# Three places for the values on their way out, and an earlier time for the second block's statistics, in the prologue of a two-layer diffusion transformer kernel

## The chip, the cores and the metric

The kernel runs on one core of one Trainium2 chip. The metric is the device time of one execution in microseconds; the time of a kernel is the median of its runs. Besides the runs there is one profiled execution, whose trace gives every instruction's start and length. The engines are PE (matrix products; PEld is its weight load), DVE (vector), ACT (scalar, activations), POOL (GpSimd) and SP, which in this kernel issues every DMA.

## The reference

The reference computes two transformer layers over 1024 latent tokens (a grid of 16 x 64) and 256 context tokens of width 1024, in float32. Layer 0 mixes by neighbourhood attention with 16 heads of 64, layer 1 by grouped-query attention. Only the start of layer 0 bears on this change:

```python
mod_l = (silu_c @ ada_w[i] + ada_b[i])[:, None, :]
sh1_l, sc1_l, g1_l, sh2_l, sc2_l, g2_l = jnp.split(mod_l, N_MOD, axis=-1)
a_l = ada_norm(h, norm_mix[i], sh1_l, sc1_l)      # rms_norm(x, g) * (1 + scale) + shift
...
qkv = a_l @ w_qkv                                  # split into q, k, v
s_nb = q_r . k_b * scale + bias                    # bias gathered from rpb
p = softmax(concat(s_nb, s_cx)); o = p @ v
y_lat = o @ w_o
...
h = h + g1_l * y_l
h = h + g2_l * swiglu_ffn(ada_norm(h, norm_ffn[i], sh2_l, sc2_l), ffn_w_in[i], ffn_w_out[i])
```

The context tokens go through the same steps with modulation vectors of their own.

## The kernel before

All matrix operands are split into a high part, rounded to the fp32r format of PE, and a low part that holds the rest, so a product takes three matmuls: high by high, low by high, high by low. Names ending in `h` and `l` are these parts (`ah`/`al` of the activations, `wh`/`wl` of the weights, `qh`/`ql` of q and k). Making the high part is a cast on ACT, making the low part a subtraction on DVE or POOL.

Tokens lie in three blocks: block 0 and block 1 are 512 latent tokens each, block 2 is the context with 256. Activations are kept with the width on the partitions, as eight slices `kc` of 128 by the block's tokens.

The prologue, `startup()`, does the following for layer 0 and for the first two heads' q and k and the first four heads' v:

- `loads()` starts all input DMAs in a fixed order, on SP.
- `stat(b)` squares the eight slices of block b on ACT (line 364; the first two are `nacc` and `nacb`, the others `nsq` with two places), adds them up on DVE (slices 2, 4, 5, 7) and POOL (slices 3, 6) at line 367, sums over partitions with a matmul pair by a matrix of ones (line 374, tile `ms`), and takes Ln and Exp on ACT (lines 377, 378) for the reciprocal root `nrs`.
- `modulation(m)` and `shift(m, w)` make the modulation vectors (lines 396, 397, 409 to 419).
- `apply0(kc)` (lines 429 to 433) and `apply(b, kc)` (lines 441, 442 and `norm_lo`, lines 131 to 134) normalize a slice: DVE makes `nx`, ACT makes `ah`, and the low part `al` is made by DVE for even slices and by POOL for odd ones, where it takes two rows (lines 131 and 132). `nx` has three places.
- `split(k, pool)` makes `wh` on ACT (line 337) and `wl` on DVE (line 339) for a weight tile; the values' weights are the two tiles `v0` and `v1`.
- `projections()` issues PE's work: q and k of block 0 (lines 781 to 783), values of tiles 0 to 3, q and k of block 1, values of tiles 4 and 5, q and k of the context block, values of tiles 8, 9, 6, 7. A tile of values is 128 tokens.
- `proj_v` makes one tile of values (lines 797 to 799) and sends it out: the cast on ACT (line 803) and the subtraction on DVE (line 804) fill a tile `vt`, and a DMA stores it in DRAM (`Vd`). The q and k parts go out in the same way from `qh` and `ql` (lines 823, 825; `Kd`, `Qd`).
- `bias_steps()` has SP issue 24 DMAs that spread the relative bias table into `E`, and 16 that gather it into `Bd`. They stand in SP's queue between the stores.

Every step of the prologue is a Python generator that yields how long, in microseconds of an assumed clock, it takes until the next step. `startup` keeps them in a heap by that clock, and the order in which they are popped is the order in which the instructions are issued on each engine. Each engine runs its instructions in that order and waits at the head of its queue for what that instruction needs. The clock decides the order alone, not the time. The start times are these:

```python
for at, gen in [(0.0, loads()), (5.0, c_rows()), (10.0, stat(0)), (CFG["t1"], stat(1)), (CFG["t2"], stat(2)), (28.0, projections())] + \
        [(CFG["ts"], shifts_ctx())] + \
        [(max(9.5, a), modulation(m)) for m, a in enumerate((7.0, 13.0, 18.0, 22.0, 25.0, 28.5, 31.5, 34.5))]:
    start(at, gen)
```

Tiles come from pools. With `bufs=2` a name has two places, which are used in turn; an instruction that writes a tile waits until whatever read or wrote the tile that last had the place is done, a store by DMA included.

After the prologue the attention of layer 0 runs by a written table (ORDERA and ORDERB), with the remaining projections and the modulation for later (`adaw`, line 503) put between by `Lanes`. Softmax blocks `Pt` are scaled by POOL (line 871), transposed on PE (line 878) and multiplied by the values (line 508). SP's place for each DMA there comes from the order in which the program, on its assumed clock, finds it ready.

Of the kernel before, what the change touches and what calls it, by code (L numbers as in the profile page):

```python
# [11 lines left out]
F32R = mybir.dt.float32r  # L12
# [6 lines left out]
P = 128  # L19
# [12 lines left out]

V_NMIX, V_NFFN, V_NFIN, V_B, V_QG, V_KG, V_C = 0, 16, 32, 40, 136, 137, 138
V_N = 154
CFG = dict(lag=3, tv=5.0, tm=5.0, t1=40.0, t2=55.0, ts=43.0, p0=28, lo="GD", n=39, ra=2.3, rc=0.7, rq=1.1, rb=1.05, gap=263, r1=1.262, lh=300, tk='ADAG', tb=1000000000.0, tg=1, lp='GD')
PERIOD1 = 8172
ORDER1 = {
# [35 lines left out]
def _build(tc, nc, I, O, top):  # L73
# [193 lines left out]
    def startup():  # L267

        ET = mybir.EngineType
        with ExitStack() as ph:  # L270
# [10 lines left out]
            def start(at, gen):  # L281

                heapq.heappush(todo, (at, next(count), gen))
# [10 lines left out]
            def load_raw(k, src):  # L294
                raws[k] = wraw.tile([P, D], F32, name="wr")
                if k[0] == "v":
                    dma(out=raws[k][:].rearrange("p (u n) -> p u n", u=2), in_=src.rearrange("u p n -> p u n"))
                else:
                    dma(out=raws[k][:], in_=src)

            def loads():
# [12 lines left out]
                for i in range(2):  # L314
                    load_raw(f"v{i}", W[16:18, :, i * 512:i * 512 + 512])
                    start(now + CFG["tv"], split(f"v{i}", w0))
                    yield 1.5
# [15 lines left out]
            def split(k, pool):  # L333
                hi = pool.tile([P, D], F32R, name="wh")
                lo = pool.tile([P, D], F32R, name="wl")
                ws[k] = hi, lo
                s.copy(hi[:], raws[k][:])
                yield 1.2
                v.tensor_tensor(lo[:], raws[k][:], hi[:].bitcast(F32), ALU.subtract)
# [4 lines left out]
            def c_rows():  # L344
                for w in range(2):
                    for i in range(2):
                        ps = psm.tile([P, 512], F32, name="ps1")
                        dg = tmp.tile([P, 4, P], F32, name="nsq", bufs=2)
                        v.tensor_tensor(dg[:], ident[:].unsqueeze(1).broadcast_to([P, 4, P]),
                                        silc2[:, 4 * i:4 * i + 4, w:w + 1].broadcast_to([P, 4, P]), ALU.mult)  # L350
                        t.matmul(ps[:], lhsT=ones[:], rhs=dg[:].rearrange("p a n -> p (a n)"), start=True, stop=True)
                        yield 0.8
                        s.mul(crow[w][:, i * 512:i * 512 + 512], ps[:], float(D))
                        yield 0.3

            def stat(b):
                n = BLK[b][1]
                acc = []
                for kc in range(KC):
# [10 lines left out]
                    yield 0.55  # L370
                yield CFG["tm"] if b == 1 else 2.0
                ms = psp.tile([P, 512], F32, name="ms")
# [26 lines left out]
            def shifts_ctx():  # L399

                for m in range(4, KC):
                    shift(m, 1)
                    yield 1.6
# [43 lines left out]
            def first_qk(b):  # L447
# [3 lines left out]
                for kc in range(KC):  # L451
                    while (b, kc) not in ready or b == 0 and min(kc + CFG["lag"], KC - 1) not in ready:
                        yield 0.2
# [7 lines left out]
            def vals0(tiles):  # L461
                for c in proj_v(psm, tmp, [ws["v0"], ws["v1"]], Vd[0], tiles):
                    yield c * 0.64
# [91 lines left out]
    class Lanes:  # L555
# [170 lines left out]
        def tick(self, cost=1.0):  # L726

            self.now += 650
            for e in "TML" + CFG["tk"]:
                if self.busy.get(e, 0) < self.now + CFG["tg" if e == "G" else "tb"]:  # L730
# [55 lines left out]
    def proj_v(psm, pool, ws, dst, tiles=range(10)):  # L786


        for tb in tiles:
            b = min(tb // 4, 2)  # L790
            ah, al = acts[b]
            c = slice((tb % 4) * P, (tb % 4) * P + P)
            ps = psm.tile([P, 512], F32, name="ps1")
            out = ps[:, :256]
            for kc in range(KC):
                hi, lo = (w.rearrange("p (u k n) -> p k u n", u=2, n=P)[:, kc % 4] for w in ws[kc // 4])
                t.matmul(out, lhsT=ah[:, kc, c], rhs=hi, start=kc == 0, stop=False)
                t.matmul(out, lhsT=al[:, kc, c], rhs=hi, start=False, stop=False)
                t.matmul(out, lhsT=ah[:, kc, c], rhs=lo, start=False, stop=kc == KC - 1)
                yield 0.5  # L800
            vt = pool.tile([P, 4, P], F32R, name="vt", bufs=2)
            pv = out.rearrange("p (h d) -> p h d", d=HD)
            s.copy(vt[:, :, 0:HD], pv)
            v.tensor_tensor(vt[:, :, HD:], pv, vt[:, :, 0:HD].bitcast(F32), ALU.subtract)
            dma(out=dst[:, :, tb, :].rearrange("h p d -> p h d"), in_=vt[:])
# [985 lines left out]
    with ExitStack() as ph:  # L1791
# [260 lines left out]
        n = CFG["n"]  # L2052
# [604 lines left out]
```

## Time and profile before

| | us |
|---|---|
| three runs | 3013.36, 3013.57, 3020.36 |
| median | 3013.57 |
| profiled execution | 3018.95 |
| its span, first to last instruction | 3017.1 |
| PE busy in the span | 2915.8 (97%) |
| DVE, ACT, POOL busy | 2300.5, 1621.0, 1238.8 |
| granted clock of PE over the span | 0.992 |

The rows of the trace are read as follows: the start in us from the span's start, the length in us, the engine, the line of the program, the operation, what it writes and reads, its shape, and how many rows are merged (x2). In brackets stands the idle time of the engine just before, and what ended it. Rows on an engine may overlap by about 0.1 us, since an instruction starts while the one ahead drains. SPq are the DMAs that SP issues; the length there is the time of issue, not of the transfer.

### The profile page before, as it was taken

The numbers are of one execution on the slowest core, as the hardware profiler recorded it, in microseconds if no ns is written. First come the engines' busy times: TensorE is split into PE (matmuls) and PEld (weight loads), VectorE is DVE, ScalarE is ACT, GpSimd is POOL, SyncE is SP. The second block draws the span as 40 slices with busy tenths as digits, with TensorE's granted clock in tenths as the row PEclk, the third lists the DMA queues.
The fourth block names the chain that finished last, engine by engine and source line by source line (L and its number), as shares of the span: only waits on it lengthen the run. The fifth ranks groups of instructions, "written<-read, shape, count | busy, mean of one in ns | idle before, by whom it ended". The sixth has DMA issues, their size and how long they took to land.

```text
span 3017.1 us, 50132 instructions
## 1 busy us (share of the span) xinstructions
PE 2915.8 (97%) x16460; PEld 2503.3 (83%) x16460; DVE 2300.5 (76%) x4671; ACT 1621.0 (54%) x3739; POOL 1238.8 (41%) x1105
## 2 busy tenths in 40 slices
PE   7999998999999999999999899999999999999998
PEld 5788997888788888888888788888888878888886
DVE  7478778876798875557777588999887887776776
ACT  4345545776742222234456489899887632333444
POOL 4246556776145451121121256666643354223112
PEclk9999999999999999999999999999999999999999
DMA  7777777887545562249656523333323343224962
GB/s 268 217 223 239 227 217 230 239 244 219 187 147 188 194 225 76 93 152 324 211 192 205 164 83 95 112 98 102 107 75 127 133 140 122 102 105 149 324 217 108
DMA packets 309218, 519.03 MB, mean 172 GB/s; under 512 B 46560, under 2 KB 113248, under 8 KB 308320
## 3 DMA queue, kind: packets, MB, share of 16 engines
q1 hardware_dynamic: 308960, 515.84, 52.7%
q8 instruction: 131, 2.15, 0.3%
q14 instruction: 127, 1.04, 0.1%
HBM read 389.61 MB, written 120.18 MB: 169 GB/s over the span
## 4 chain that ended last, share of the span: by engine, by line
PE 77%; DVE 10%; DMA 4%; ACT 3%; POOL 2%; issue 2%; SPq 1%; DVEq 0%; ACTq 0%; POOLq 0%
PE pf L1472 9%; PE pf L1474 9%; PE pf L1473 9%; PE T L878 5%; PE o L508 5%; PE pf L1721 5%; PE pf L1720 5%; PE pf L1722 5%; PE ps L781 3%; PE ps L783 3%; PE ps L782 3%; PE S L2265 2%; PE S L2266 2%; DVE pT L891 1%; PE pf L1494 1%
## 5 line engine op out<-in xcount | busy, mean ns | idle before, releaser
L871 POOL TENSOR_SCALAR Pt<-Pt,rc 128x1280 f32<-128x1280 f32 (+3 forms) x288 | 298.0, 1035 | 390.3 <-ACT pT L886 144.3
L891 DVE TENSOR_TENSOR pT<-T,pT 128x256 fp32r<-128x256 f32 (+2 forms) x672 | 341.9, 535 | 34.3 <-ACT pT L886 33.8
L886 ACT CAST pT<-T 128x256 fp32r<-128x256 f32 (+2 forms) x672 | 304.5, 477 | 111.9 <-PE T L878 107.5
L878 PE MATMUL T<-ident,Pt 128*128 128x128 f32 x1952 | 302.8, 274 | 24.1 <-POOL Pt L871 23.5
L878 PEld LDWEIGHTS T<-ident,Pt 128*128 128x128 f32 x1952 | 234.7, 140 | 80.7 <-POOL Pt L871 36.9
L508 PE MATMUL o<-pT,Vt 128*128 128x256 f32 x1952 | 295.2, 289 | 2.5 <-DVE pT L891 2.5
L781 PE MATMUL ps<-ah,wh 128*128 128x512 f32 (+1 forms) x688 | 261.2, 380 | 8.0 <-ACT ah L442 4.1
L508 PEld LDWEIGHTS o<-pT,Vt 128*128 128x128 f32 x1952 | 253.8, 189 | 9.9 <-DVE pT L891 6.2
L782 PE MATMUL ps<-al,wh 128*128 128x512 f32 (+1 forms) x688 | 251.3, 365 | 3.0 <-POOL al L132 2.3
L860 ACT ACTIVATE Pt<-S,rc 128x512 f32<-128x512 f32 (+2 forms) x384 | 247.1, 654 | 9.6 <-DVE rc L852 6.4
L783 PE MATMUL ps<-ah,wl 128*128 128x512 f32 (+1 forms) x688 | 250.7, 364 | 0.0
L2257 DVE TENSOR_REDUCE nm<-S 128x1 f32<-128x512 f32 x256 | 169.7, 683 | 35.7 <-PE S L2266 34.0
L963 POOL TENSOR_TENSOR c<-c,c 128x512 f32<-128x512 f32 (+1 forms) x63 | 93.5, 1486 | 249.6 <-DVE c L966 80.4
L966 DVE TENSOR_TENSOR c<-c,c 128x512 fp32r<-128x512 f32 (+1 forms) x166 | 131.0, 803 | 46.4 <-ACT c L1448 33.7
L860 ACT ACTIVATE Pt<-X,rc 128x256 f32<-128x256 f32 x256 | 125.0, 488 | 67.9 <-DVE rc L852 55.1
L1448 ACT CAST wh<-c 128x512 fp32r<-128x512 f32 x112 | 68.8, 618 | 166.2 <-PE pf L1473 66.5
L781 PEld LDWEIGHTS ps<-ah,wh 128*128 128x128 f32 x688 | 131.4, 191 | 21.2 <-ACT ah L442 4.2
L783 PEld LDWEIGHTS ps<-ah,wl 128*128 128x128 f32 x688 | 130.9, 190 | 21.2
L1472 PE MATMUL pf<-c,wh 128*128 128x512 f32 x376 | 146.5, 390 | 0.0
L1473 PE MATMUL pf<-c,wh 128*128 128x512 f32 x376 | 146.5, 390 | 0.0
L1474 PE MATMUL pf<-c,wl 128*128 128x512 f32 x376 | 146.3, 389 | 0.0
L906 POOL TENSOR_TENSOR r<-ob 128x256 f32<-128x256 f32 x144 | 123.5, 857 | 54.7 <-ACT ob L900 53.7
(596 smaller groups left out, 9137.4 us busy)
## 6 DMA issues: line engine op xcount, KB each, us to landing
c<-in_fout SPq DMA_DIRECT2D x119, 256.0 KB, 3.9
wr<-in_wqkv SPq DMA_DIRECT2D x53, 512.0 KB, 4.8
wr<-in_adaT SPq DMA_DIRECT2D x96, 256.0 KB, 3.2
c<-in_fin SPq DMA_DIRECT2D x68, 256.0 KB, 3.0
adaw<-in_adaT SPq DMA_DIRECT2D x64, 256.0 KB, 3.9
wr<-in_wo SPq DMA_DIRECT2D x32, 512.0 KB, 4.4
wr<-in_fin SPq DMA_DIRECT2D x58, 256.0 KB, 2.7
K<-Kd SPq DMA_DIRECT2D x64, 224.0 KB, 5.2
```

The costliest lines, as they stand in the source:

```text
L508: t.matmul(o_ap, lhsT=u.V[:, kb, :], rhs=u.pT[:, i, :], start=i == 0, stop=i == len(u.blocks) - 1)
L781: t.matmul(ps, lhsT=hi[:, c], rhs=ah[:, kc, :n], start=kc == 0, stop=False)
L782: t.matmul(ps, lhsT=hi[:, c], rhs=al[:, kc, :n], start=False, stop=False)
L783: t.matmul(ps, lhsT=lo[:, c], rhs=ah[:, kc, :n], start=False, stop=kc == KC - 1)
L860: s.activation(u.Pt[:, off:off + u.wid[c]], u.S[c], AF.Exp, bias=u.min, scale=u.sign, accum_out=u.rc[:, 3 + c:4 + c])
L871: g.tensor_scalar(Pt, Pt, u.rc[:, 2:3], 1.0, ALU.mult, ALU.mult)
L878: t.transpose(T[:, i * P:(i + 1) * P], u.Pt[:, (i0 + i) * P:(i0 + i + 1) * P], ident[:])
L886: s.copy(u.pT[:, i0:i0 + n, :P], u.T[c])
L891: v.tensor_tensor(u.pT[:, i0:i0 + n, P:], u.T[c], u.pT[:, i0:i0 + n, :P].bitcast(F32), ALU.subtract)
L1472: t.matmul(ps[:], lhsT=r32(hi[:, c]), rhs=bh, start=k == 0, stop=False)
L1473: t.matmul(ps[:], lhsT=r32(hi[:, c]), rhs=bl, start=False, stop=False)
L1474: t.matmul(ps[:], lhsT=r32(lo[:, c]), rhs=bh, start=False, stop=k == 3)
```

## The change

Two numbers of the configuration and one count of places change:

```diff
-CFG = dict(lag=3, tv=5.0, tm=5.0, t1=40.0, t2=55.0, ts=43.0, p0=28, ...)
+CFG = dict(lag=3, tv=5.0, tm=5.0, t1=37.0, t2=53.0, ts=43.0, p0=28, ...)
...
-            vt = pool.tile([P, 4, P], F32R, name="vt", bufs=2)
+            vt = pool.tile([P, 4, P], F32R, name="vt", bufs=3)
```

`t1` is the time on the assumed clock at which the statistics of block 1 start, `t2` that of the context block's. The instructions stay the same; their order moves on the engines. On ACT, between the last slices of block 0 and the first q and k parts (`wh<-wr` are the casts of the values' weights, `x_166` is block 1, `x_165` block 0):

```order
 L337 CAST wh<-wr 128x1024
+L364 ACTIVATE nacc<-x_166 128x512
 L429 ACTIVATE ah_326<-x_165,modA_82,G_0_86 128x512
+L364 ACTIVATE nacb<-x_166 128x512
+L364 ACTIVATE nsq<-x_166 128x512
 L337 CAST wh<-wr 128x1024
-L364 ACTIVATE nacc<-x_166 128x512
-L364 ACTIVATE nacb<-x_166 128x512
-L364 ACTIVATE nsq<-x_166 128x512 x2
+L364 ACTIVATE nsq<-x_166 128x512 x5
 L823 ACTIVATE qh<-ps_408 128x512
```

Three of block 1's squares now stand ahead of the second cast of the values' weights, and all eight ahead of the first `qh`. On DVE at the same place (`wl` are the weights' low parts, `al_327` the last slice of block 0, `ql` the first low part of k):

```order
+L367 TENSOR_TENSOR nacc<-nacc,nsq 128x512
 L339 TENSOR_TENSOR wl<-wr,wh 128x1024
 L433 TENSOR_TENSOR al_327<-nx,ah_326 128x512
+L367 TENSOR_TENSOR nacc<-nacc,nsq 128x512
 L339 TENSOR_TENSOR wl<-wr,wh 128x1024
-L367 TENSOR_TENSOR nacc<-nacc,nsq 128x512
+L367 TENSOR_TENSOR nacc<-nacc,nsq 128x512 x2
 L825 SCALAR_TENSOR_TENSOR ql<-ps_408,qh 128x512
```

The first addition of block 1's squares moves ahead of both low parts of the values' weights and of block 0's last `al`.

On DVE some twenty rows later, where block 1's normalization begins (`vt<-ps_633` and `vt<-ps_671` are the third and fourth tile of values, `nx` the normalized slices). Before:

```order
L804 TENSOR_TENSOR vt<-ps_633,vt 128x4x64
L804 TENSOR_TENSOR vt<-ps_671,vt 128x4x64
L441 SCALAR_TENSOR_TENSOR nx<-x_166,G_0_86,nrs 128x512 x2
L134 SCALAR_TENSOR_TENSOR al_696<-nx,modA_82,ah_695 128x512
L441 SCALAR_TENSOR_TENSOR nx<-x_166,G_0_86,nrs 128x512 x2
```

And now, where the same two tiles are `ps_636` and `ps_679`:

```order
L441 SCALAR_TENSOR_TENSOR nx<-x_166,G_0_86,nrs 128x512
L804 TENSOR_TENSOR vt<-ps_636,vt 128x4x64
L441 SCALAR_TENSOR_TENSOR nx<-x_166,G_0_86,nrs 128x512
L134 SCALAR_TENSOR_TENSOR al_658<-nx,modA_82,ah_657 128x512
L441 SCALAR_TENSOR_TENSOR nx<-x_166,G_0_86,nrs 128x512
L804 TENSOR_TENSOR vt<-ps_679,vt 128x4x64
```

The two tiles of values now come behind the first and the third `nx`. On ACT the casts for them moved in the same way, behind the first and the third `ah` of block 1. On PE the matmul pair for block 1's sum moved from the third tile of values to the second, behind six of its eight steps. On POOL the two 128x256 additions of the context block's squares, which stood ahead of slice 3's and slice 5's `al`, now both stand ahead of slice 5's.

On SP, from the stores of block 1's q (`Qd_92<-ql`) to the first loads of the attention:

```order
 L81 DMA Qd_92<-ql 128x512
-L81 DMA E<-in_rpbp 16x31x8
-L81 DMA Bd<-E 16x24x128 x3
+L81 DMA E<-in_rpbp 16x31x8 x3
 L81 DMA Vd_108<-vt 128x4x128
-L81 DMA Bd<-E 16x24x128 x3
+L81 DMA Bd<-E 16x24x128 x4
 L81 DMA Vd_108<-vt 128x4x128
 L81 DMA Bd<-E 16x24x128 x9
```

and behind the stores of the context block's q and k:

```order
-L81 DMA Bd<-E 16x24x128
-L81 DMA Vd_108<-vt 128x4x128 x2
-L81 DMA wr<-in_wqkv 128x1024 x2
-L81 DMA Vd_108<-vt 128x4x128 x2
+L81 DMA Bd<-E 16x24x128 x3
+L81 DMA Vd_108<-vt 128x4x128 x3
+L81 DMA wr<-in_wqkv 128x1024
+L81 DMA Vd_108<-vt 128x4x128
+L81 DMA wr<-in_wqkv 128x1024
 L81 DMA Qs<-Qd_92 64x768 x2
```

Two of the E loads moved behind the stores of block 1's q and k, three of the Bd rows instead of one stand behind the context block's, and the second weight load stands behind the last store of values. Further on, up to the 344th of SP's 2,169 rows, some loads and stores of the attention change places with a neighbour.

More of the change, by code (lines that the diff above doesn't have):

```diff
@@ L34 @@
 V_N = 154
-CFG = dict(lag=3, tv=5.0, tm=5.0, t1=40.0, t2=55.0, ts=43.0, p0=28, lo="GD", n=39, ra=2.3, rc=0.7, rq=1.1, rb=1.05, gap=263, r1=1.262, lh=300, tk='ADAG', tb=1000000000.0, tg=1, lp='GD')
+CFG = dict(lag=3, tv=5.0, tm=5.0, t1=37.0, t2=53.0, ts=43.0, p0=28, lo="GD", n=39, ra=2.3, rc=0.7, rq=1.1, rb=1.05, gap=263, r1=1.262, lh=300, tk='ADAG', tb=1000000000.0, tg=1, lp='GD')
 PERIOD1 = 8172
```

## The prediction

> **What bounds the kernel now.** The page comes first: the span, the busy shares, and the chain of what ended last, 77% of which lies on PE.
>
> ```profile
> span 3017.1 us, 50132 instructions
> PE 2915.8 (97%) x16460; PEld 2503.3 (83%) x16460; DVE 2300.5 (76%) x4671; ACT 1621.0 (54%) x3739; POOL 1238.8 (41%) x1105
> ```
>
> PE is the bound, so what the change is worth is read from PE's idle time in the stretch that it touches. The table of stretches (length, then busy time and count by engine, then the granted clock) gives it:
>
> ```profile
> 37.00:68.00 31.00, 29.57 (x183) 23.84 (x181) 22.93 (x44) 13.52 (x24) 15.30 (x10) 0.98 0.75 266
> 68.00:90.00 22.00, 15.03 (x52) 10.05 (x53) 15.69 (x19) 10.05 (x22) 11.88 (x10) 0.92 0.47 73
> ...
> 114.00:140.00 26.00, 23.44 (x128) 20.37 (x128) 7.39 (x19) 5.63 (x13) 2.22 (x3) 1.00 0.91 291
> 140.00:340.00 200.00, 191.95 (x1336) 178.47 (x1337) 157.52 (x442) 99.01 (x294) 102.76 (x116) 0.97 0.74 226
> ```
>
> Length less PE's busy time leaves 1.4 us idle in 37 to 68, 7.0 in 68 to 90, 2.6 in 114 to 140 and 8.0 in 140 to 340. All the idle time that the change could touch directly is thus about 11 us, 0.4% of the span. The timeline of PE shows where it lies (start, length, in brackets the idle time before and its releaser):
>
> ```profile
> 53.65 0.39 PE L782 MATMUL ps<-al,wh 128*128 128x512 f32 x1
> ...
> 67.58 0.28 PE L799 MATMUL ps<-wl,ah 128*128 128x256 f32 x1
> 71.91 0.50 PE L781 MATMUL ps<-ah,wh 128*128 128x512 f32 x1 [4.05 <-ACT ah L442]
> 72.69 0.80 PE L782 MATMUL ps<-al,wh 128*128 128x512 f32 x1 [0.29 <-DVE al L134]
> ...
> 85.43 0.50 PE L782 MATMUL ps<-al,wh 128*128 128x512 f32 x1 [0.88 <-POOL al L132]
> ...
> 88.91 0.50 PE L782 MATMUL ps<-al,wh 128*128 128x512 f32 x1 [0.46 <-POOL al L132]
> ...
> 114.14 0.50 PE L781 MATMUL ps<-ah,wh 128*128 128x512 f32 x1 [1.10 <-DVE vt L804]
> ...
> 140.51 0.93 PE L878 MATMUL T<-ident,Pt 128*128 128x128 f32 x4 [2.92 <-POOL Pt L871]
> ```
>
> Row 53.65 is the first matmul to read the last `al` slice of block 0. At 67.58 the values of tiles 0 to 3 end, and PE stands 4.05 us for block 1's normalized input. Its q and k projections then stop at 85.43 and 88.91 for POOL's `al`. At 114.14 PE waits for a `vt`, and at 140.51 for the first softmax block of the attention. The engines behind these waits:
>
> ```profile
> 48.92 1.04 ACT L337 CAST wh<-wr 128x1024 fp32r<-128x1024 f32 x1
> ...
> 51.52 0.62 ACT L364 ACTIVATE nacc<-x 128x512 f32<-128x512 f32 x1
> ...
> 66.16 0.63 ACT L378 ACTIVATE nrs<-nrs 128x512 f32<-128x512 f32 x1
> 69.61 0.37 ACT L803 CAST vt<-ps 128x256 fp32r<-128x256 f32 x1 [2.81 <-DMA Vd<-vt]
> ...
> 113.26 0.37 ACT L803 CAST vt<-ps 128x256 fp32r<-128x256 f32 x1 [5.46 <-DMA Vd<-vt]
> ...
> 132.74 0.60 ACT L823 ACTIVATE qh<-ps 128x512 fp32r<-128x512 f32 x1 [8.65 <-DMA Qd<-qh]
> ```
> ```profile
> 51.75 0.69 DVE L433 TENSOR_TENSOR al<-nx,ah 128x512 fp32r<-128x512 f32 x1 [0.51 <-POOL nx L431]
> ...
> 62.18 1.22 DVE L396 CUSTOM_DVE_ANT_0 adaj<-ash,crow 128x1024 f32<-128x1024 f32 x1
> 63.57 0.41 DVE L804 TENSOR_TENSOR vt<-ps,vt 128x256 fp32r<-128x256 f32 x1
> ...
> 70.36 1.41 DVE L441 SCALAR_TENSOR_TENSOR nx<-x,G,nrs 128x512 f32<-128x512 f32 x2
> 71.89 0.75 DVE L134 SCALAR_TENSOR_TENSOR al<-nx,modA,ah 128x512 fp32r<-128x512 f32 x1
> ...
> 138.60 0.69 DVE L503 CUSTOM_DVE_ANT_0 adaj<-adaw,crow 128x512 f32<-128x512 f32 x1 [3.31 <-DMA adaw<-in_adaT]
> ```
>
> ACT has block 1's rs at 66.79, but its next row is the cast of the fourth `vt`, which stands until 69.61 for the DMA that empties the place of the second. DVE's subtraction for that cast is queued ahead of the first nx, so nx starts at 70.36. That is the wait that the third place removes. The row at 113.26 is the same wait for the ninth tile.
>
> **The change, part by part.** (a) *Statistics ahead of the weights' conversions* (t1 from 40 to 37). On ACT three squares and the last `ah0` now stand between the two `wh` casts. The first cast stays at 48.92; kc2's square, the fourth row behind it, ends near 52.2 (a square is 0.62 long and the rows overlap by 0.1; 48.92 to 51.52 holds two casts and `ah0`, so that `ah0` takes 0.7). On DVE the addition of that square now heads the queue: it holds the first `wl` and block 0's last `al`, which need nothing from it. The addition (0.69, as `al` of the same shape in row 51.75) runs from 52.3, the next row from 52.9, `wl` to 54.04, `al` from there to 54.73 in place of 51.75 to 52.44. Row 53.65 waits for it: PE loses 1.1 us, and the values end at 69.0 instead of 67.86. The second `wl`, near 56.5, is read by the first tile's fifth step at about 57.3 and is covered.
>
> (b) *The statistics themselves.* There are two `nsq` places, so the later squares wait for the additions that empty them; POOL's two additions count.
>
> ```profile
> 53.80 1.54 POOL L367 TENSOR_TENSOR nacb<-nacb,nsq 128x512 f32<-128x512 f32 x1 [2.08 <-ACT nsq L364]
> ...
> 72.62 1.83 POOL L131 TENSOR_SCALAR nx<-nx,modA 128x512 f32<-128x512 f32 x1 [12.63 <-ACT ah L442]
> ...
> 86.78 0.69 POOL L131 TENSOR_SCALAR nx<-nx,modA 128x512 f32<-128x512 f32 x1 [1.40 <-ACT ah L442]
> 87.55 1.30 POOL L132 TENSOR_TENSOR al<-nx,ah 128x512 fp32r<-128x512 f32 x1
> ```
>
> With 1.54 for POOL's addition (row 53.80; DVE works beside it here too): kc3's 53.8 to 55.3, kc6's square 55.9 to 56.5, its addition to 58.1, kc7's square to 58.7, DVE's last addition to 59.5. The q and k casts now wait behind kc7's square; with their two subtractions (0.69 each) DVE is free at 60.6. Four shifts at 1.39 (62.18 to 63.57, with two short followers in it) and two `vt` subtractions at 0.34 (0.41, overlapping) bring it to 66.8. The matmul pair for the sum stands six steps into the second tile, so rs is ready near 65.2 and DVE's own queue decides: the first nx starts at 66.8, 3.5 us earlier than 70.36.
>
> (c) *Up to the end of block 1's q and k.* From nx to the end of `al` took 2.28 us (70.36 to 72.64). Now the third tile's cast (0.37) and subtraction (0.42) stand in between, and DVE waits for the cast: 3.6 us, so `al` is there at 70.4 and PE's second matmul starts there instead of 72.69. PE's gap shrinks from 4.05 to about 1 us. On POOL both 128x256 additions now stand behind kc3's pair and ahead of kc5's. kc3's `al` gains 0.9 us by that; kc5's must wait for the square of kc6 of the third block, which ACT makes only after `ah1` of kc6. Followed through with 0.85 for the pair's first row on POOL (nearer to 0.69 than to 1.83, since of DVE's rows beside it only one nx is long) and 1.30 for the subtraction, that square ends at 81.1, the addition at 81.9, kc5's `al` at 84.1. PE goes on at 84.15 instead of 85.43; the matmuls from there to kc7's take 2.9 us, which is past kc7's `al` (86.2). So block 1 ends 1.8 us earlier (87.1 against 88.91).
>
> (d) *SP.* From here SP's queue matters as much as PE:
>
> ```profile
> 71.43 12.90 SPq L81 DMA_DIRECT2D E<-in_rpbp  x19
> 90.59 0.34 SPq L81 DMA_DIRECT2D Kd<-qh  x1
> ...
> 92.68 0.54 SPq L81 DMA_DIRECT2D E<-in_rpbp  x1
> 95.12 1.84 SPq L81 DMA_DIRECT2D Bd<-E  x3
> ...
> 100.24 6.49 SPq L81 DMA_DIRECT2D Bd<-E  x9
> ...
> 114.12 1.24 SPq L81 DMA_DIRECT2D Vd<-vt  x2
> 115.40 1.20 SPq L81 DMA_DIRECT2D Qs<-Qd  x2
> ```
> ```profile
> 109.53 3.64 DMA Vd<-vt
> ...
> 124.73 7.89 DMA Qd<-qh
> ```
>
> SP idles from 84.3 until the store of block 1's k at 90.59, which now comes at 88.8. Behind it stand three E rows instead of one (0.68 each from row 71.43, +1.36 us) and the same sixteen Bd rows; the first Bd waits about 2.4 us from the last E's issue (92.68 to 95.12). Counted down the new order, the store of the seventh `vt` goes out at 108.6 (109.53 before), the eighth and ninth, no longer held by a place, by 110.2. The tenth `vt` shares its place with the seventh, whose DMA lands 3.64 us after issue, at 112.2: cast, subtraction and store follow at 113.2, then a weight load, then the first Qs at 114.2. Before it was 115.40. SP gains 1.2 us.
>
> (e) *Which of the two arrives.* PE, 1.8 us ahead and without the 1.10 us wait at 114.14 (the ninth `vt` no longer waits for the seventh's DMA), runs 3.0 us ahead from 111.1. But the wait at 140.51 is not released by PE's work: the store of q (124.73, landing after 7.89 us) frees the buffer for ACT's row 132.74, then SP's adaw load, DVE's 138.60 and POOL's Pt follow. All of it is counted from SP's Qs. So 1.2 of the 3.0 us arrive and the wait of 2.92 us grows to about 4.7.
>
> (f) *The rest.* From 140 on the order on PE, DVE, ACT and POOL is the old one. On SP a few loads change neighbours until about 340 us. I take zero for it: the loads that swap are the next heads' K, Q and adaw. Its ends are 8 us of gain (all of PE's idle time in that stretch) and three waits like the 2.92 us one lost.
>
> The sum: -1.1 and +3.5 in the statistics become +1.8 at the end of block 1, +3.0 on PE, +1.2 where SP decides. The profiled execution took 3018.95 us, 1.85 more than its span; it would take 3017.7. It lies 5.4 us above the median of the three runs (3013.57), which by the same step gives 3012.4. No change below 0.3% (9 us) can be told from none here.
>
> **Rivals.** *PE's lead arrives whole.* If the tenth `vt` doesn't hold SP, Qs goes out near 112.0, 3.4 us early, and PE's 3.0 becomes the limit: 3010.5. For it: such stores land after 2.3 us at best (min, median, max of the `vt` stores):
>
> ```profile
> DMA to landing us min/median/max: 2.3/3.7/5.6
> ```
>
> Against it: the tenth cast has no other place to go to, and even 2.3 us leaves half of the wait.
>
> *Slower: POOL's kc5 pair.* It now waits behind an addition that depends on ACT and DVE. From 85.4 on it decides: if `al` of kc5 comes 1.3 us later than counted, block 1 ends no earlier than before and SP has its 1.36 us more: Qs at 116.8, the time 3015.0. For it: the pair's first row took 1.83 us at 72.62 beside DVE's nx pair (70.36's successor), 0.69 at 86.78 with DVE idle; now an addition and an nx of DVE fall at just that moment. Against it: the subtraction behind it took 1.30 at 87.55, and DVE's rows of 128x256 are short. [...]
>
> *SP's new order reaches the attention.* A DVE row that waits for adaw, as at 138.60 for 3.31 us, could be won or lost two or three times before 340: 3006 or 3021.
>
> **How the numbers follow.** My sum 0.45 (3011 to 3014), PE's lead 0.2, POOL's pair 0.2, SP's order 0.15, a little more of it on the gaining side since 8 us of idle time lie there. 3006 to 3018 leaves out the ends of the last case and some of the runs' own spread (3013.36 to 3020.36). Only that case can pass 9 us: faster 0.07, slower 0.04, the same 0.89.
>
> **What would show it.** Right: block 0's last `al` near 54.7 behind an addition; no ACT wait for a `Vd` store before nx, nx near 67; PE's gap before block 1 near 1 us and a granted clock above the 0.92 of 68 to 90; no wait near 111 for a `vt`; Qs near 114; T near 139.3 behind a longer wait. Wrong: nx not before 69, kc5's `al` after 85.4, or the difference found beyond 340.

## The result: slower, by 4 to 9 us

The changed kernel is slower. Its median is 3025.67 us over 20 runs, that of the kernel before, run beside it, 3016.47 us over 20: a ratio of 1.0029 (95% interval 1.0023 to 1.0035), about 9 us. One of the 20 took 5856 us; like the few such runs below it is left out of the ratio. On another chip (experiment 15) the ratio was 1.0013 (1.0000 to 1.0026), about 4 us. The forecast was 3012.4 us and no measurable change, with nothing under 0.3% to be told from none; the first interval is 0.12% wide. Some 3 us of the miss lie in its base: the three runs that were shown have a median of 3013.57, twenty of the same kernel one of 3016.47.

The profiled execution after has a span of 3024.4 us (3017.1 before). PE's stretches, with the columns as before:

```profile
37.00:68.00 31.00, 26.51 (x146) 20.53 (x146) 22.95 (x42) 12.47 (x22) 14.18 (x10) 0.94 0.66 241
68.00:90.00 22.00, 16.57 (x79) 12.71 (x79) 15.88 (x23) 10.65 (x23) 10.37 (x10) 0.87 0.55 106
...
114.00:140.00 26.00, 24.47 (x140) 21.40 (x139) 6.16 (x13) 4.93 (x12) 1.99 (x2) 1.00 0.99 299
140.00:340.00 200.00, 186.16 (x1315) 173.18 (x1314) 154.76 (x438) 97.72 (x291) 102.12 (x115) 0.99 0.76 230
```

PE lost 3.1 us of busy time in 37 to 68 (26.51 against 29.57) and got 1.5 back in 68 to 90. In 114 to 140 it looks the busier one, and in 140 to 340 it has 5.8 us less (186.16 against 191.95): 2.6 of it because the wait ahead of the attention's first transpose, which lay just ahead of 140.51, now lies just ahead of 144.54, the rest in longer waits of the transposes (line 878) up to 245 us. The granted clock there is 0.99 against 0.97, and on balance PE lost nothing more: it was 4.0 us late at the transpose and 3.9 at 340 us. PE's waits in the timeline of the changed kernel:

```profile
56.70 0.50 PE L782 MATMUL ps<-al,wh 128*128 128x512 f32 x1 [2.01 <-DVE al L433]
...
72.42 0.28 PE L799 MATMUL ps<-wl,ah 128*128 128x256 f32 x1
72.54 0.39 PE L781 MATMUL ps<-ah,wh 128*128 128x512 f32 x1
...
75.41 0.50 PE L782 MATMUL ps<-al,wh 128*128 128x512 f32 x1 [0.94 <-POOL al L132]
...
79.21 0.50 PE L782 MATMUL ps<-al,wh 128*128 128x512 f32 x1 [0.77 <-POOL al L132]
...
82.82 0.51 PE L782 MATMUL ps<-al,wh 128*128 128x512 f32 x1 [1.95 <-DVE al L134]
...
86.03 1.22 PE L374 MATMUL ms<-nacc,ones 128*128 128x256 f32 x2 [1.77 <-DVE nacc L367]
...
144.54 0.65 PE L878 MATMUL T<-ident,Pt 128*128 128x128 f32 x4 [3.07 <-POOL Pt L871]
```

The wait of 4.05 us ahead of block 1 is gone: its first matmul (72.54) comes straight behind the values. But that is mostly because PE itself came late. The values end at 72.70 and not at 67.86, and block 1 starts 0.6 us later than before (72.54 against 71.91). There is a new wait of 2.01 us for block 0's last `al` at 56.70, and behind it PE ran at half its clock (0.51 granted from 57.11 to 60.53, last section). Within block 1 the waits for `al` are 0.94, 0.77 and 1.95 us, and PE now also waits 1.77 us for the sum of block 2's squares, whose matmul pair stands in the middle of block 1's: 5.4 us together, where the kernel before had 3.0 behind its first matmul. The engines behind it, DVE, then ACT, then POOL, then SP (rows on an engine overlap by about 0.1 us: DVE's row of 53.15 ends at 53.84, its next one starts at 53.75):

```profile
53.15 0.69 DVE L367 TENSOR_TENSOR nacc<-nacc,nsq 128x512 f32<-128x512 f32 x1 [2.47 <-ACT nsq L364]
...
54.89 1.75 DVE L433 TENSOR_TENSOR al<-nx,ah 128x512 fp32r<-128x512 f32 x1
...
67.49 0.42 DVE L804 TENSOR_TENSOR vt<-ps,vt 128x256 fp32r<-128x256 f32 x1 [0.89 <-ACT vt L803]
...
69.22 0.74 DVE L441 SCALAR_TENSOR_TENSOR nx<-x,G,nrs 128x512 f32<-128x512 f32 x1
...
81.68 0.43 DVE L367 TENSOR_TENSOR nacc<-nacc,nsq 128x256 f32<-128x256 f32 x1 [1.09 <-ACT nsq L364]
82.02 0.75 DVE L134 SCALAR_TENSOR_TENSOR al<-nx,modA,ah 128x512 fp32r<-128x512 f32 x1
```
```profile
67.08 0.37 ACT L803 CAST vt<-ps 128x256 fp32r<-128x256 f32 x1 [4.17 <-PE ps L799]
...
68.08 0.63 ACT L378 ACTIVATE nrs<-nrs 128x512 f32<-128x512 f32 x1
...
117.47 0.37 ACT L803 CAST vt<-ps 128x256 fp32r<-128x256 f32 x1 [3.38 <-DMA Vd<-vt]
```
```profile
54.66 1.43 POOL L367 TENSOR_TENSOR nacb<-nacb,nsq 128x512 f32<-128x512 f32 x1 [3.11 <-ACT nsq L364]
...
84.97 0.72 POOL L367 TENSOR_TENSOR nacb<-nacb,nsq 128x256 f32<-128x256 f32 x1 [4.93 <-ACT nsq L364]
85.67 0.86 POOL L131 TENSOR_SCALAR nx<-nx,modA 128x512 f32<-128x512 f32 x1
86.61 1.59 POOL L132 TENSOR_TENSOR al<-nx,ah 128x512 fp32r<-128x512 f32 x1
```
```profile
93.76 0.34 SPq L81 DMA_DIRECT2D Kd<-qh  x1
...
119.29 1.14 SPq L81 DMA_DIRECT2D Qs<-Qd  x2
...
129.55 0.38 SPq L81 DMA_DIRECT2D Qd<-qh  x1
```

Block 0's `al` (54.89) took 1.75 us instead of 0.69. Block 1's first nx came at 69.22 (70.36 before). `al` of kc4 (82.02) stands behind an addition that waits for ACT's square, and POOL's pair for kc5 (85.67, 86.61) behind one that waited 4.93 us for a square, so that kc5's `al` was there at 88.20. An addition stood ahead of kc5's pair before as well, but it waited for less, and `al` was there at 85.37:

```profile
82.11 0.73 POOL L367 TENSOR_TENSOR nacb<-nacb,nsq 128x256 f32<-128x256 f32 x1 [2.62 <-ACT nsq L364]
82.83 0.86 POOL L131 TENSOR_SCALAR nx<-nx,modA 128x512 f32<-128x512 f32 x1
83.77 1.60 POOL L132 TENSOR_TENSOR al<-nx,ah 128x512 fp32r<-128x512 f32 x1
```

Block 1's k went out at 93.76 (90.59 before), SP's first Qs at 119.29 (115.40), the first transpose of the attention came at 144.54 (140.51).

### The profile page after: what moved, and what is told of

The parts are those of the page before. It is cut to its first block, busy times and chain, and to the rows that moved or that the text cites. A ratio compares the mean times of both kernels' runs of the same rounds, so it can differ in the third digit from the quotient of the medians.

```text
span 3024.4 us, 50130 instructions
## 1 busy us (share of the span) xinstructions
PE 2914.6 (96%) x16460; PEld 2502.8 (83%) x16460; DVE 2299.1 (76%) x4671; ACT 1621.6 (54%) x3739; POOL 1237.7 (41%) x1105
## 4 chain that ended last, share of the span: by engine, by line
PE 80%; DVE 8%; DMA 4%; ACT 3%; POOL 2%; issue 2%; SPq 1%; DVEq 0%; ACTq 0%; POOLq 0%
PE pf L1472 9%; PE pf L1474 9%; PE pf L1473 9%; PE T L878 6%; PE o L508 5%; PE pf L1720 5%; PE pf L1722 5%; PE pf L1721 5%; PE ps L781 3%; PE ps L782 3%; PE ps L783 3%; PE S L2265 2%; PE S L2266 2%; PE pf L1495 1%; PE pf L1494 1%
## 5 line engine op out<-in xcount | busy, mean ns | idle before, releaser
L878 PE MATMUL T<-ident,Pt 128*128 128x128 f32 x1952 | 303.0, 274 | 28.7 <-POOL Pt L871 27.9
L878 PEld LDWEIGHTS T<-ident,Pt 128*128 128x128 f32 x1952 | 234.8, 140 | 85.9 <-POOL Pt L871 41.4
L782 PEld LDWEIGHTS ps<-al,wh 128*128 128x128 f32 x688 | 131.4, 191 | 18.4 <-POOL al L132 3.0
```

The source lines that it names most:

```text
L782: t.matmul(ps, lhsT=hi[:, c], rhs=al[:, kc, :n], start=False, stop=False)
L878: t.transpose(T[:, i * P:(i + 1) * P], u.Pt[:, (i0 + i) * P:(i0 + i + 1) * P], ident[:])
```

## The experiments

Sixteen kernels ran. The ratio is always to the kernel before, run beside it on the same chip. Four chips were used: one for experiments 1 to 4, others for 5 to 8, 9 to 12 and 13 to 16. Ratios that stand beside each other on one chip compare better than others. Most rest on 10 to 12 runs, experiment 1 on 5 and experiment 4 on 6. The table has four marks of each profile: SP's store of block 1's k, SP's first Qs, PE's first transpose (T, L878), and how many us later (minus: earlier) than in the kernel before PE started the matmul that stood at 340 us there.

| kernel | k | Qs | T | at 340 | ratio (95%) |
|---|---|---|---|---|---|
| before | 90.59 | 115.40 | 140.51 | 0 | 1 |
| changed | 93.76 | 119.29 | 144.54 | 3.9 | 1.0029 (1.0023 to 1.0035) |
| 15: changed, other chip | 92.68 | 118.06 | 144.91 | 1.4 | 1.0013 (1.0000 to 1.0026) |
| 1: t2 back at 55 | 92.35 | 117.48 | 143.74 | 1.7 | 1.0045 (1.0032 to 1.0058) |
| 2: two places again | 93.89 | 119.93 | 144.17 | -1.1 | 1.0009 (1.0000 to 1.0018) |
| 3: third place alone | 89.63 | 113.94 | 138.86 | -3.1 | 1.0010 (1.0001 to 1.0019) |
| 4: t2 = 53 and place | 92.95 | 117.35 | 143.83 | 1.1 | 1.0039 (1.0028 to 1.0050) |
| 5: t1 = 38.5 and place | 93.12 | 118.51 | 144.71 | 3.6 | 1.0025 (1.0015 to 1.0036) |
| 6: before, delayed | 95.69 | 120.41 | 145.40 | 3.7 | 1.0018 (1.0009 to 1.0028) |
| 7: changed, split places | 92.33 | 118.30 | 142.44 | -4.1 | 1.0006 (0.9992 to 1.0020) |
| 16: the same, other chip | 92.25 | 118.19 | 142.91 | -3.6 | 1.0017 (1.0007 to 1.0026) |
| 8: changed, kc3's addition on DVE | 91.08 | 116.61 | 141.93 | 3.1 | 1.0023 (1.0013 to 1.0032) |
| 9: split places alone | 89.73 | 114.15 | 140.09 | -4.4 | 1.0005 (0.9994 to 1.0017) |
| 10: 5 with split places | 92.65 | 118.84 | 143.44 | -1.0 | 1.0028 (1.0016 to 1.0040) |
| 11: 4 with split places | 92.39 | 117.41 | 142.04 | -2.8 | 1.0005 (0.9992 to 1.0018) |
| 12: 1 with split places | 91.16 | 117.45 | 141.72 | -5.4 | 1.0007 (0.9994 to 1.0021) |
| 13: place and delay | 93.77 | 118.11 | 144.23 | 5.2 | 1.0007 (0.9998 to 1.0016) |
| 14: split places and delay | 94.77 | 121.04 | 146.45 | 1.9 | 1.0016 (1.0006 to 1.0026) |

**1 to 4: the change taken apart.** Theory A: the third block's statistics (t2) hold block 1's last `al`. Theories B and C: SP's new order is at fault, behind 114 us (B) or in the E rows (C).

```diff
1:  t1=37.0, t2=55.0, vt bufs=3
2:  t1=37.0, t2=53.0, vt bufs=2
3:  t1=40.0, t2=55.0, vt bufs=3
4:  t1=40.0, t2=53.0, vt bufs=3
```

> The changed kernel with t2 put back to 55: the third block's statistics stand later, so that POOL has the pair of kc5 ahead of both 128x256 additions, and DVE has kc4's al ahead of them; SP's order is that of the changed kernel. Theory A (the loss enters in 78 to 93 us, where the third block's statistics hold block 1's last al, and SP's queue carries it on): block 1's first qh near 89 to 90 us in place of 93.14, the first Qs near 115, the ratio to the kernel before 0.9990 to 1.0008. Theory B (SP's new order beyond 114 us loses it): the prologue gets faster, but the ratio stays at 1.0015 to 1.003. Theory C (the three E rows ahead of the Bd rows lose it): Qs at 116 to 119 us though block 1 ends early, ratio 1.001 to 1.003.

> The changed kernel with two places for vt again: PE, DVE, ACT and POOL keep the changed order word for word, SP has the E and Bd rows of the changed kernel but the old order of the Vd stores and of all that follows to 340 us. nx of block 1 waits for the second place's store again. Theory A: block 1's first qh near 93 to 95 us, Qs near 119 to 121, ratio 1.002 to 1.004. Theory B: ratio 0.9995 to 1.0015, because the order beyond 114 us is the old one. Theory C: as A, about 1.002.

> The kernel before with the third place alone: PE, DVE, ACT and POOL have the old order, SP's differs only from the ninth Vd store on (about 112 us). ACT's vt cast no longer waits 2.81 us for the second Vd store. Theory A: nx of block 1 up to 2 us earlier, block 1's first qh near 88 to 89, Qs 113 to 115, ratio 0.9985 to 1.0003. Theory B: the same prologue, but the loss comes between 140 and 400 us: ratio 1.001 to 1.003. Theory C: as A.

> The kernel before with the third place and t2 at 53, t1 left at 40: only the third block's statistics move; on POOL kc6's addition stands ahead of kc1's pair, and on DVE four additions stand among block 1's nx rows. Theory A: block 1 ends 1 to 3 us later than in the kernel with the third place alone, ratio 1.0005 to 1.002 against the kernel before. Theory B: as the third place alone, 1.001 to 1.003. Theory C (the E rows stand as before): 0.999 to 1.0005.

Theory A, that t2 alone is at fault, fell with the first run: with t2 back, block 1's k left only 1.4 us earlier, at 92.35, and the ratio was 1.0045 where at most 1.0008 was expected. PE's waits there are as long as in the changed kernel, and DVE's rows show that additions of the third block still stand ahead of an `al` of block 1:

```profile
56.40 0.69 PE L782 MATMUL ps<-al,wh 128*128 128x512 f32 x1 [2.01 <-DVE al L433]
...
79.79 0.50 PE L782 MATMUL ps<-al,wh 128*128 128x512 f32 x1 [1.69 <-POOL al L132]
...
85.92 0.50 PE L782 MATMUL ps<-al,wh 128*128 128x512 f32 x1 [1.75 <-DVE al L134]
```
```profile
84.78 0.42 DVE L367 TENSOR_TENSOR nacc<-nacc,nsq 128x256 f32<-128x256 f32 x1 [1.09 <-ACT nsq L364]
85.12 0.74 DVE L134 SCALAR_TENSOR_TENSOR al<-nx,modA,ah 128x512 fp32r<-128x512 f32 x1
```

The addition waits 1.09 us for ACT's square, which stands on ACT behind an `ah` that waits for DVE's nx: the two engines wait for each other in turn.

t2 alone does it too, at another place (POOL's first 128x256 addition now stands ahead of kc1's pair, and waits for its square):

```profile
77.98 0.79 PE L782 MATMUL ps<-al,wh 128*128 128x512 f32 x1 [4.58 <-POOL al L132]
```
```profile
74.69 0.72 POOL L367 TENSOR_TENSOR nacb<-nacb,nsq 128x256 f32<-128x256 f32 x1 [13.93 <-ACT nsq L364]
```

The third place alone does what it says: ACT's wait for the second Vd store is gone, block 1 starts at 70.97 and its k leaves at 89.63. It gained 1.0 us there (1.6 us of T), and none of it is seen in the time (1.0010).

These kernels ran on one chip, and two of them differ from experiment 3 in one number alone. Experiment 1 adds t1 = 37: k 2.7 us and T 4.9 us later, 1.0045 (1.0032 to 1.0058) against 1.0010 (1.0001 to 1.0019). Experiment 4 adds t2 = 53: k 3.3 us and T 5.0 us later, 1.0039 (1.0028 to 1.0050). The intervals do not touch, so each of t1 and t2 by itself makes block 1 late and, beside the third place, costs time: 9 to 11 us here, as much as the whole change on its own chip, so the two hardly add up. But experiment 2 has t1 and t2 of the change, its late block 1 (93.89) and T (144.17), with two places, and measured 1.0009. A late block 1 alone cost it nothing that its time shows. It has SP's old order behind 114 us, and so theory B stays (below). Theory C falls: experiment 2 has the new E rows and measured less than the 1.002 expected, experiment 4 has the old ones and is slow.

**5, 8: which part of t1.** Experiment 5 moves t1 only so far that block 0's `al` and the first `wl` stay ahead of the statistics; experiment 8 takes POOL's addition from beside that `al`.

```diff
5:  t1=38.5, t2=55.0, vt bufs=3
8:  (the changed kernel)
-   (v, g)[i].tensor_tensor(acc[i][:], acc[i][:], sq[:], ALU.add)
+   (v, g)[i and (b, kc) != (1, 3)].tensor_tensor(acc[i][:], acc[i][:], sq[:], ALU.add)
```

> The third place with t1 at 38.5 and t2 at 55: the second block's statistics stand behind block 0's last al and the first wl, but still ahead of the second wl and of the q and k casts. Theory L (what is late in the prologue arrives whole through SP's first Qs): no wait of PE for al of L433 at 56 us (2.01 us with t1 at 37), no half-rate window near 57, block 1's first matmul at 69.5 to 70.5, its first qh store at 88 to 89, Qs at 112.5 to 114, ratio to the kernel before 0.9980 to 1.0003. Theory O (SP's order of the third place loses it beyond 114): the same prologue, ratio 1.001 to 1.003. Theory G (the loss is half-rate windows that the waits of the prologue set off): as L, with one or two half-rate windows less than in the changed kernel up to 200 us.

> The changed kernel with one addition of the second block's statistics (kc3's) on DVE in place of POOL; it stands on DVE right behind block 0's last al, which took 1.75 us beside POOL's addition and 0.69 us in the kernel before. Theory G: al takes 0.7 us, PE's wait for it falls from 2.01 to about 1.0 us, the half-rate window near 57 us goes, PE is 2 to 2.5 us earlier at 68, nx near 68.5, ratio 1.0010 to 1.0022. Theory L: the wait at 56 shrinks likewise, but block 1's end is still held by al of kc4 and kc5, so that Qs moves by under 1 us: ratio 1.002 to 1.003.

Experiment 5 has no wait at 56 us, and block 1's first matmul came at 69.52, 2.4 us ahead of the kernel before. But then PE waited 2.07 us for POOL and 3.46 us for DVE, and k left at 93.12, not at 88 to 89 as theory L had it. The last of these waits is again an addition ahead of an `al`, which then ran beside POOL and took 1.77 us:

```profile
82.74 0.50 PE L782 MATMUL ps<-al,wh 128*128 128x512 f32 x1 [2.07 <-POOL al L132]
...
87.85 0.50 PE L782 MATMUL ps<-al,wh 128*128 128x512 f32 x1 [3.46 <-DVE al L134]
```
```profile
85.38 0.72 DVE L367 TENSOR_TENSOR nacc<-nacc,nsq 128x256 f32<-128x256 f32 x1 [1.09 <-ACT nsq L364]
86.02 1.77 DVE L134 SCALAR_TENSOR_TENSOR al<-nx,modA,ah 128x512 fp32r<-128x512 f32 x1
```

An early start was worth nothing, because the additions came among block 1's rows with it.

Experiment 8 settles why block 0's `al` took 1.75 us. With the addition on DVE it takes 0.69 us again; the next addition that runs beside POOL's takes 1.78:

```profile
54.70 0.69 DVE L433 TENSOR_TENSOR al<-nx,ah 128x512 fp32r<-128x512 f32 x1
...
57.64 1.78 DVE L367 TENSOR_TENSOR nacc<-nacc,nsq 128x512 f32<-128x512 f32 x1
```
```profile
57.34 1.54 POOL L367 TENSOR_TENSOR nacb<-nacb,nsq 128x512 f32<-128x512 f32 x1 [5.97 <-ACT nsq L364]
```
```profile
55.44 0.50 PE L782 MATMUL ps<-al,wh 128*128 128x512 f32 x1 [0.94 <-DVE al L433]
```

In both kernels the long DVE row started behind POOL's (54.89 behind 54.66, 57.64 behind 57.34) and ended about 0.55 us behind it (56.64 behind 56.09, 59.42 behind 58.88). PE's wait fell from 2.01 to 0.94 us, near the 1.1 that the prediction had counted with an undisturbed `al`, and PE's half-rate stretch behind it is gone. T came 2.6 us earlier than in the changed kernel. The ratio of 1.0023 cannot be told from either of the changed kernel's two, and theory G (the loss is half-rate stretches), which had 1.0010 to 1.0022, is neither shown nor ruled out by it.

**6, 13, 14: does a late block 1 arrive?** Every queue in its order, but six more rows of 0.7 us on DVE ahead of block 1 (6 in the kernel before, 13 in experiment 3, 14 in experiment 9):

```diff
-   v.scalar_tensor_tensor(x[:], xs[b][:, kc, :], G1[0][:, kc, w:w + 1], rs[b][:], ALU.mult, ALU.mult)
+   for _ in range(7 if (b, kc) == (1, 0) else 1): v.scalar_tensor_tensor(x[:], ...)
```

> The kernel before in its old order on every queue, with DVE's first nx of block 1 computed seven times instead of once (6 rows of 0.7 us, 4.2 us in all; the value is the same). Theory L: block 1 starts and ends about 4.2 us later, Qs near 119.5, ratio 1.0010 to 1.0016, as much as the changed kernel lost by 340 us in its profile. Theory O: the old order takes up a part of it in the attention's first waits, ratio 1.0000 to 1.0008. Theory G: the longer gap (8 us in place of 4) costs one half-rate window more, 1.0014 to 1.0022.

In experiment 6 it arrives: k 5.1 us later, Qs 5.0, T 4.9, and the time by 0.18%, 5.5 us (2.7 to 8.5), as much as the change costs (4 to 9 us). The delay brought a slower PE with it: PE waited 8.49 us ahead of block 1 and then ran at half its clock for 13.7 us, where the kernel before did so for 3.4 (0.50 granted from 72.49 to 75.90). The same delay in experiments 13 and 14 made T 5.4 and 6.4 us later than in 3 and 9, and the ratios are 1.0007 against 1.0010 and 1.0016 against 1.0005, on different chips. So one measurement of three shows the cost clearly. Over the table T and the ratio go together loosely: the two kernels with an early block 1 (3 and 9) have a mean T of 139.5 and a mean ratio of 1.0008, the fifteen measurements with a late one 143.8 and 1.0019, but these range from 1.0005 to 1.0045 with little order by T (14 has the latest T, 146.45, and 1.0016; 13 has 144.23 and 1.0007).

**7, 9 to 12, 15, 16: SP's order.** The place also changes about a hundred entries of SP's queue from the ninth Vd store to about 340 us. Giving tiles 2 and 5 a place of their own keeps the place and restores SP's old order there, with the four other queues word for word as they were:

```diff
-   vt = pool.tile([P, 4, P], F32R, name="vt", bufs=3)
+   vt = pool.tile([P, 4, P], F32R, name="vu" if tb in (2, 5) else "vt", bufs=1 if tb in (2, 5) else 2)
```

> The changed kernel with the third place for the first six tiles alone: tiles 2 and 5 use a place of their own, the others share two. The prologue up to 110 us stands as in the changed kernel on every engine, while SP has, from the ninth Vd store on, the old order of the kernel before. Theory L: block 1's first qh store near 93.8, ratio 1.002 to 1.0035 as the changed kernel. Theory O: ratio 0.9995 to 1.0015, as the changed kernel with two places. Theory G: as L.

> The kernel before with a place of their own for tiles 2 and 5 of the values, t1 and t2 unchanged: every queue, SP's too, keeps the old order; only ACT's wait for the second Vd store (2.81 us) goes. Against the third place alone (1.0010) it differs in nothing but SP's order from the ninth Vd store on. Theory O (that order costs 3 to 6 us): ratio 0.9983 to 1.0000, T after the q projections at most 140 us, idle time of PE from 200 to 270 us near 2.6 us, not above 3.3. Theory L (only lateness before 115 us counts): as the third place alone, 1.0003 to 1.0018.

> The kernel with t1 at 38.5 and three places (1.0025), its late SP order set back to the old one by giving tiles 2 and 5 a place of their own; the other four queues keep their order word for word. Theory O: 3 to 6 us less, ratio 1.0003 to 1.0015, Qs near 118 still, PE's idle time from 200 to 270 us near 2.6 in place of 6.0 us. Theory L: ratio 1.0015 to 1.0035.

> The kernel with t2 at 53 and three places (1.0039), SP's order set back in the same way; block 1's q and k end 2 us later than in the kernel before. Theory O: ratio 1.0008 to 1.0025, idle from 200 to 270 us near 2.6 in place of 4.4 us. Theory L: 1.0028 to 1.0050.

> The kernel with t1 at 37, t2 at 55 and three places (1.0045), SP's order from the ninth Vd store on set back in the same way. Theory O: ratio 1.0010 to 1.0030, idle from 200 to 270 us near 2.6 in place of 3.9 us. Theory L: 1.0032 to 1.0058.

In experiments 1 to 12 this looked like the answer: the changed kernel fell from 1.0029 to 1.0006, experiment 1 from 1.0045 to 1.0007, 4 from 1.0039 to 1.0005, all three under what theory L allows (and 11 and 12 even under theory O). But 3 and 5 hardly moved (1.0010 to 1.0005, 1.0025 to 1.0028), and experiments 9 and 10 missed theory O, which had at most 1.0000 and 1.0015 for them. The trace shows an effect as well. In the new order one of two weight loads leaves straight ahead of the first Qs and K, and the eight K loads then took 5.36 to 7.71 us to issue, in the old order 5.07 or 5.08 in every profile (the changed kernel, then experiment 7):

```profile
118.74 0.50 SPq L81 DMA_DIRECT2D wr<-in_wqkv  x1
119.29 1.14 SPq L81 DMA_DIRECT2D Qs<-Qd  x2
120.47 5.96 SPq L81 DMA_DIRECT2D K<-Kd  x8
```
```profile
113.50 1.57 SPq L81 DMA_DIRECT2D wr<-in_wqkv  x2
117.30 0.94 SPq L81 DMA_DIRECT2D Vd<-vt  x2
118.30 1.47 SPq L81 DMA_DIRECT2D Qs<-Qd  x2
119.82 5.07 SPq L81 DMA_DIRECT2D K<-Kd  x8
```

But the two kernels of a pair had not run on one chip. Experiments 13 to 16 are two pairs on one:

> The third place alone (1.0010) with DVE's first nx of block 1 computed seven times instead of once: t1 and t2 as before, the prologue 4.2 us later by plain work, SP's late order the new one. Theory O2 (SP's new order costs nothing while the prologue is early, and 4 to 10 us once it is late, since then the second load of the next weights leaves just ahead of the first Qs and K loads): the eight K loads take 5.8 to 7.3 us to issue in place of 5.07, PE's idle time from 200 to 270 us 3.3 to 6, ratio 1.0030 to 1.0050. Theory A2 (order and lateness only add up: 0.0005 and 0.0018): ratio 1.0015 to 1.0028. Theory L (lateness alone): 1.0012 to 1.0022.

> The same delay with tiles 2 and 5 in a place of their own, so that SP's late order is the old one; every other queue reads word for word as in the kernel with the third place and the delay. Theory O2: eight K loads in 5.07 us, ratio 1.0005 to 1.0018. Theory A2: 1.0012 to 1.0022. Theory L: the same as its partner, 1.0012 to 1.0022.

> The changed kernel once more, to stand on one chip with its partner below. Theory O2: 1.0023 to 1.0035. Theory L: the same.

> The changed kernel with tiles 2 and 5 in a place of their own, beside the changed kernel on one chip: the two differ in 102 places of SP's queue from the ninth Vd store on, and in nothing else. Theory O2: 1.0000 to 1.0014, at least 0.0012 under its partner. Theory L: within 0.0008 of its partner.

There the new order is not the slower one: 1.0007 (13) against 1.0016 (14) with the delay, 1.0013 (15) against 1.0017 (16) with the change. Theory O2 missed 13, 15 and 16; theory L was right on 14 and 16 and missed 13 and 15, which were faster than either had them. A part of what O rested on were differences between chips: the changed kernel itself measured 1.0029 on one chip and 1.0013 on another, and its partner 1.0006 and 1.0017.

That does not settle it, for two reasons. On the chip of experiments 1 to 4 the late kernels with the new order (1.0045 and 1.0039) stand clear of the late one with the old order (1.0009), and they ran side by side. And the traces side with the new order as the slower one. In all seven pairs (changed and 7, 15 and 16, 1 and 12, 4 and 11, 5 and 10, 3 and 9, 13 and 14) PE is later at 340 us with the new order than with the old, by 1.3 to 8.0 us, though the stores of k are at most 1.4 us apart. Between the two matmuls that stood at 200 and 270 us before, PE was idle for 2.18 to 2.96 us in the ten profiles with the old order and for 3.29 to 6.00 us in the eight with the new one. These are single executions, and PE's half-rate stretches fall differently in each (between 50 and 150 us they start at 57.1, 84.4 and 145.8 in the first profile of the change, at 72.5 and 140.8 in that of the kernel before). Whether SP's new order costs time, and when, stays open.

## Why the prediction was wrong, step by step

(a) *The statistics ahead of the weights' conversions*: right in kind, mis-sized. DVE's addition headed the queue at 53.15 and held `wl` and `al`, but `al` was taken at 0.69 us from a row that ran alone; beside POOL's addition (54.66, 1.43 us) it took 1.75. PE lost 2.01 us, not 1.1, and then, in the first profile, ran for 3.4 us at half its clock (0.51 granted), which the sum has at nothing. The prediction had taken POOL's row (1.54) from one with DVE at work beside it, and DVE's from one that ran alone. What it had noted of POOL, 1.83 us beside DVE's nx pair and 0.69 with DVE idle, was seen on DVE too: its rows that started behind a POOL addition took 1.75 us here and 1.78 in experiment 8, and ended 0.55 and 0.54 us after that addition.

(b) *nx at 66.8*: failed, it came at 69.22. The additions and casts ran 1.5 us behind the count (DVE was free at 62.10, not at 60.6), of which 0.9 us was late already at a small matmul (line 417, 49.94 against 49.06) ahead of anything that moved. The other 0.9 us of nx's lateness are PE's: between the shifts DVE's queue holds the subtraction of the second tile's values (67.49), which waited for ACT's cast (67.08), and that for PE, which was late by (a). The reciprocal root, whose matmul pair stands in the same tile, was there only at 68.71. Counting a queue's own rows was not enough: one row in it belonged to the engine that (a) had delayed.

(c) *Block 1 ends 1.8 us earlier*: wrong in sign, and this is the step that decides. The gap of 4.05 us closed, but by PE's own lateness: the values ended 4.8 us later, and block 1 started 0.6 us later than before where the sum had its second matmul 2.3 us earlier. Within block 1 the sum allowed 0.5 us more than before, and PE's waits alone grew by 2.4 us: kc3's `al` gained 0.35 us where 0.9 was counted, kc4's stood behind an addition (1.95 us of PE's time), and PE itself waited 1.77 us for block 2's sum, which the prediction did not price at all. The signs that were named said so: nx came after 69, and the granted clock of 68 to 90 was 0.87, not above 0.92. The rival "POOL's kc5 pair" named a hold of the right kind, and kc5's `al` did pass its limit (88.20 against 85.4). But PE, held by the other two and at half its clock from 84.4 (0.50 granted to 91.2), reached it only at 88.32 and did not stand for it. The rival had a chance of 0.2 and a price of 2.6 us. Against 88.8 for the store of k stand 93.76 and 92.68 in the two profiles of the change.

(d) *SP*: right. From the store of k to Qs 25.4 us were counted (88.8 to 114.2) and 25.53 measured (93.76 to 119.29; before 24.81), the tenth `vt` waiting 3.38 us for a Vd store as forecast. (e) *Only SP's part arrives*: the same, 25.1 counted from Qs to T, 25.25 measured, with a wait of 3.07 us at T in place of the 4.7. The chain behind block 1 up to T was understood; what was fed into it was off by 5.0 us at the store of k and had the wrong sign.

(f) *The rest is zero*: not shown either way. For SP's order the seven pairs above speak against zero up to 340 us, the two timed on one chip do not. The start of the same matmul, counted back from the last one, lay 3.9 us behind the kernel before at 340 us and 7.3 at the end in the first profile of the change, 1.4 and 3.8 in the second. On PE, DVE, ACT and POOL no instruction changed its order there. PE's half-rate stretches (below) fall differently in each execution, but they are not the answer by themselves: they add up to 49 us in the first profile and 56 in the second, and the second is the shorter one (3020.9 us against 3024.4).

Put right, the steps give about 3 us more at block 1's k (2.3 of the order's own), 0.7 on SP, 4.0 at T, and that is the loss of the second measurement (1.0013); that the two agree is partly luck, since experiments 2 and 13 were as late at T and lost less. The first measurement has 5 us more, and where they come from stays open. SP's order behind 114 us is the nearest rival; and the same program differs by 0.0011 to 0.0016 between chips.

## What to carry to other kernels

Work pulled forward in an engine's queue was paid here by whatever it was put in front of (2.01 us of PE's time at block 0's `al`, 1.95 at kc4's): every row that waited there, an addition for its square above all, became a wait of the rows behind it. So list for each pulled row the instructions that it now holds, on every engine and on the one that the program is bound by too. A row's duration from a trace holds for the company in which it ran (block 0's `al` took 0.69 us alone and 1.75 beside POOL's addition). A gap that closes is no gain until it is seen which side of it moved. And two kernels that are to be compared within 0.3% have to run beside each other on one chip: three of five pairs measured apart agreed on a cause that two pairs measured together did not confirm.

## What the runs showed of the hardware

In the profiles the clock granted to PE was full or half (1.0 or 0.5) and changed on a grid of 3.41 us: the profiles of the kernel before and of the change hold 42 intervals at one rate, and all but the last of each, where the record ends, are 1 to 250 times 3.413 us long. A wait of 2 us could be enough to halve the next 3.41 us: the new one of 2.01 us at 56.70 did it in the changed kernel (PE busy and, behind the counts, the granted clock; the kernel of experiment 8, with its shorter wait, below):

```profile
53.70:57.11 3.41, 1.40 (x7) 0.85 (x6) 3.41 (x4) 2.03 (x4) 1.43 (x1) 0.99 0.87 301
57.11:60.53 3.42, 3.42 (x14) 3.03 (x13) 3.27 (x4) 1.61 (x3) 1.47 (x1) 0.51 0.02 7
```
```profile
52.70:56.10 3.40, 2.46 (x11) 1.70 (x11) 3.15 (x5) 2.29 (x5) 0.00 (x0) 1.00 0.65 225
56.10:59.50 3.40, 3.40 (x28) 3.26 (x27) 3.33 (x3) 1.74 (x4) 1.54 (x1) 1.00 0.27 88
```

With this grid laid over all 18 profiles, as far as the record of the clock goes: at full rate a stretch with PE busy for less than 40% was followed by half rate 104 times in 104, one of 40 to 52% 66 times in 104, one above 52% never in some 15,400. At half rate a stretch below 80% was followed by half rate every time (55), one above 88% once in 154. So half rate stayed here until a nearly full stretch, and each one at half rate cost up to 1.7 us (an estimate: half of 3.41). Where the grid stood differed between executions: a boundary lay at 57.1 in the first profile of the change and at 56.25 in that of experiment 15. There the same wait of 2.02 us left PE busy for 1.48 of the stretch's 3.41 us, and the next one ran at full rate. The kernel before spread over 3010.51 to 3028.08 us beside experiments 13 to 16. That the grid is one source of this spread is likely and not shown.
